# Packed softmax statistics, a spread over 128 rows and another order of the last tile in a three-mixer decoder trunk

## The chip, the cores and the metric

The kernel runs on one core of a Trainium2 chip. A core has five engines, each with a queue of its own: TensorE (PE; its weight loads are shown as PEld), VectorE (DVE), ScalarE (ACT), GpSimd (POOL) and SyncE (SP), which here issues the transfers. The metric is the device time in microseconds, median of three runs.

## The reference

A sequence of 512 rows of width 1024 goes through one layer: a root-mean-square norm, one wide projection, three mixers side by side, their gated sum and an output projection that is added to the input.

```
hn = rms_norm(x, ln_g[l])
proj = einsum('bsd,dc->bsc', hn, w_in[l])
qa, ka, va, ga, qb, kb, vb, gb, qc, kc, vc, gc, gate_logits = split(proj)
o_a = moba_attention(...)        # mixer A, 8 heads of 64
o_b = dilated_attention(...)     # mixer B, three groups of 8 heads
o_c = swa_sink_attention(...)    # mixer C, 8 heads, 2 for keys and values
branches = stack([o_a * silu(ga), o_b * silu(gb), o_c * silu(gc)])
br = einsum('bsiw,iwd->bsid', branches, w_branch[l])
x = x + einsum('bsd,de->bse', sum(sigmoid(gate_logits) * br), w_out[l])
```

Mixer B has three groups with (window, dilation) = (128, 1), (512, 4), (2048, 16). For each position and head the outputs of the groups are mixed by the softmax of their log-sum-exps, so the kernel needs from each group a maximum and a sum of exponentials for each position and head, and then one factor for each.

## The kernel before

All of the large products are made in three parts: a number is split into a high part and the rest (`whi`, `wlo` for a weight, `xhi`, `xlo` for the input), and high times high, low times high and high times low are added. So each column of a projection `pj` is made of triples of matmuls, lines 492, 493 and 494.

The input is normed in four token tiles of 128 rows. For each, ACT squares and sums (L208), DVE makes `rvx` (L141), POOL raises it to the power -0.5 (`rrx`, L143), DVE scales (`xn`, L213), PE transposes (L219, into `pt` and `xsc`), ACT and DVE split the result into `xhi` and `xlo` (L132, L137).

The mixers run in ten units, `A0 W0 R0 Z0 A1 W1 R1 Z1 C0 C1`: half the heads each, W, R and Z for the three groups of mixer B. The projection of the next unit is put between the steps of a unit. In what order the instructions stand on each engine is decided by a scheduler, which runs the kernel on its own estimates of durations; a changed instruction can move others that it has nothing to do with.

Softmax statistics lie in two tiles, `sl` (sums) and `sm` (minima of the negated maxima), of 128 rows by 4 token tiles by 96 columns: group W at columns 0 to 7, R at 32 to 39, Z at 64 to 71. R and Z compute their queries in a permuted order of tokens. After each third unit of mixer B comes a merge (L948 to L987): the statistics are transposed (`trs`, L953), copied back in the order of the tokens (`un`, L957), transposed again (`trb`, L960) and copied (L961); then come the factors. There are two merges, after Z0 and after Z1.

`spread` (L780 to L806) brings factors, one for each head and token, to the rows of the outputs: they are split into high and low parts in `ws`, transposed (L796), copied into a tile `wst`, and multiplied by a table of ones, `emat`, in a matmul `pb` (L805) with 64 rows of contraction. Groups 0 and 1 lie in the lower and upper 64 rows of one `wst`, group 2 in another. A and C call it with one value, the merge with three, so there are 20 matmuls `pb`.

The last projection keeps eight accumulators `acc`, one for each token tile and column half; it does the first six of eight slices of contraction for all of them, and then the last two, token tile by token tile (`out_mm`, L1084 to L1100). DVE adds the input to each half (`xr`, L1106) and SP stores it.

Of the kernel before, what the change touches and what calls it, by code (L numbers as in the profile page):

```python
# [9 lines left out]
F32 = mybir.dt.float32  # L10
F32R = mybir.dt.float32r
# [6 lines left out]
S = 512  # L18
D = 1024
NT = 4  # L20
KT = 8
# [4 lines left out]
ORAWS = 3  # L26
LAG = 2
KEEP = 0
UNITS = ("A0", "W0", "R0", "Z0", "A1", "W1", "R1", "Z1", "C0", "C1")
# [33 lines left out]
def shape_constants():  # L63
# [21 lines left out]
    ident[np.arange(128), 255 - np.arange(128)] = 1.0  # L85
    em = np.zeros((128, 512), np.float32)
    for g in range(4):
        for h in range(8):
            em[32 * g + h, h * 64 : (h + 1) * 64] = 1.0
    oh = np.concatenate([oh, oh])  # L90
# [10 lines left out]
def body(tc, x, ln_g, w_in, qk_g, sinks, w_branch, w_out, rel_bias, c_ident, c_onehot, c_mask, c_expand, out):  # L101
    nc = tc.nc
# [8 lines left out]
    with top:  # L111
# [7 lines left out]
        xlo = cp.tile([128, KT, S], F32R, name="xlo")  # L119
        emat = cp.tile([128, 512], F32R, name="emat")  # L120
        mhalf = cp.tile([128, 8], F32, name="mhalf")
# [104 lines left out]
        def start_bias():  # L226
# [9 lines left out]
            for kinds in (("A", "W"), ("C", "R", "Z")):  # L236
# [16 lines left out]
                nc.sync.dma_start(scr[:, c0 : c0 + n], fb[:, :n])  # L253
            e32 = qkv.tile([128, 512], F32, name="e32", tag="qn", bufs=3)
            nc.sync.dma_start(e32, c_expand)
            V.tensor_copy(emat, e32)

# [178 lines left out]
        with att:  # L436
# [7 lines left out]
            for c in range(0, 192, 32):  # L444
                G.tensor_copy(ws[:, :, c : c + 32], zer.rearrange("p (t c) -> p t c", t=NT))
            pthi = at.tile([128, 1664], F32R, name="pthi", bufs=1)
            ptlo = at.tile([128, 1664], F32R, name="ptlo", bufs=1)
# [333 lines left out]
            def spread(vals, hf, order, use):  # L781
# [9 lines left out]
                wst = []  # L791
                for g0 in range(0, ng, 2):
                    n = 64 * min(2, ng - g0)
                    tr = ps.tile([128, NT, 128], F32R, name="trs", tag="po")
                    for t in range(NT):
                        T.transpose(tr[:n, t], ws[:, t, 64 * g0 : 64 * g0 + n], order)  # L796
                    wt = at.tile([128, S], F32R, name="wst", tag="wst", bufs=2)
                    V.tensor_copy(wt[:n], tr[:n].bitcast(F32).rearrange("p a b -> p (a b)"))
                    wst.append(wt)
                for p in range(2):  # L800
                    for g in range(ng):
                        rows = slice(64 * (g % 2), 64 * (g % 2) + 64)
                        pb = ps.tile([128, 512], F32, name="pb", tag="po")
                        es = emat[rows, (hf * 2 + p) * 128 : (hf * 2 + p + 1) * 128]
                        T.matmul(pb, es, wst[g // 2][rows, :], start=True, stop=True)  # L805
                        use(p, g, pb)  # L806

            def stat_tile(tag, bufs):
                st = at.tile([128, NT, 96], F32, name=tag, tag=tag, bufs=bufs)
                G.memset(st, 0.0)  # L810
                return st

            def stat_fn(sl, sm, hf, g):
                def f(t, j):
                    c = 32 * g + hf * 4 + j
                    return sl[:, t, c : c + 1], sm[:, t, c : c + 1]

                return f
# [68 lines left out]
            for ui, (kind, hf, gi) in enumerate(units):  # L887
# [18 lines left out]
                else:  # L906
                    sl = stat_tile("sl", 2)
                    sm = sl[:, :, 32:]
                stat = stat_fn(sl, sm, hf, gi)
                steps = (residue_attention if kind in "RZ" else shared_attention if kind == "C" else pair_attention)(kind, hf, u, stat, oraw)  # L910
# [37 lines left out]
                elif len(bstate["o"]) == 3:  # L948

                    for s_ in (sl, sm):  # L950
                        tr = ps.tile([96, NT, 128], F32, name="trs", tag="po")
                        for t in range(NT):
                            T.transpose(tr[:, t], s_[:, t], rev)  # L953
                        un = at.tile([96, S], F32, name="un", tag="bt")
                        for g, pm in enumerate("NRR"):
                            rows = slice(32 * g, 32 * g + 32)
                            A.copy(perm_view(un[rows, :], pm), tr[rows])  # L957
                        tb = ps.tile([128, NT, 96], F32, name="trb", tag="po")
                        for t in range(NT):
                            T.transpose(tb[:, t], un[:, t * 128 : (t + 1) * 128], ident[:96, :96])  # L960
                        V.tensor_copy(s_, tb)  # L961
                    ln, mn = sl, sm
                    cs = [slice(32 * g + hf * 4, 32 * g + hf * 4 + 4) for g in range(3)]
                    mm = at.tile([128, NT, 4], F32, name="mm", tag="mm")
# [118 lines left out]
        wo = wnext  # L1083
        def out_mm(k, t):  # L1084
            tsl = slice(t * 128, (t + 1) * 128)
            for part, ws in ((mhi, (0, 1)), (mlo, (0,))):
                for e in range(2):
                    es = slice(e * 512, e * 512 + 512)
# [9 lines left out]
        for t in range(NT):  # L1098
            for k in range(KT - 2, KT):
                out_mm(k, t)  # L1100
        for t in range(NT):
# [29 lines left out]
```

## Time and profile before

| what | value |
|---|---|
| median of three runs | 805.29 us (805.21 to 806.34) |
| profiled execution | 808.76 us, its span 807.0 us |
| busy PE, DVE, ACT, POOL | 97%, 64%, 54%, 16% of the span |
| mean granted clock of TensorE | 0.987 |

The span reaches from the first to the last instruction of the profiled execution; 1.76 us of it lie outside. Busy shares are means over stages that differ, and PE is busy in nearly all of them.

### The profile page before, as it was taken

What the parts mean: (1) busy time and instruction counts of PE and PEld (TensorE: products, weight loads), DVE (VectorE), ACT (ScalarE), POOL (GpSimd) and SP (SyncE); (2) the same over time, 40 slices, a digit from 0 to 9 for tenths busy, and PEclk for the clock granted to TensorE, in tenths of its full rate; (3) what the DMA queues carried; (4) which work ended last, traced back from release to release, by engine and by line L of the source; (5) the groups of instructions that cost most, each with busy time, mean ns of one, the idle gap of its engine ahead of it and who ended that gap; (6) DMA issues with size and microseconds to landing.
All of it is one profiled execution on the core that took longest, in us unless ns stands there. A gap on an engine that the chain in (4) does not pass through costs nothing.

```text
span 807.0 us, 12636 instructions
## 1 busy us (share of the span) xinstructions
PE 783.0 (97%) x4727; PEld 663.4 (82%) x4727; DVE 515.6 (64%) x1088; ACT 432.4 (54%) x938; POOL 128.2 (16%) x90
## 2 busy tenths in 40 slices
PE   7999999999998999999999899999999999999997
PEld 4887887788878777878887787788899999999886
DVE  6765664564554667346554486848889887987512
ACT  5534564666577356447775865766355244445300
POOL 5422211112310340122032042100000000000000
PEclk9999999999998999999999699999999999999999
DMA  9443343351331153414431221414143334436302
GB/s 280 126 150 85 103 121 102 106 168 35 105 111 27 52 157 79 142 46 147 131 105 33 80 65 42 154 54 137 46 157 123 90 102 131 131 101 201 117 1 104
DMA packets 67328, 85.72 MB, mean 106 GB/s; under 512 B 4899, under 2 KB 53155, under 8 KB 67268
## 3 DMA queue, kind: packets, MB, share of 16 engines
q1 hardware_dynamic: 67268, 84.93, 34.2%
q8 instruction: 37, 0.61, 0.3%
q14 instruction: 23, 0.19, 0.1%
HBM read 75.41 MB, written 9.50 MB: 105 GB/s over the span
## 4 chain that ended last, share of the span: by engine, by line
PE 88%; DVE 4%; ACT 4%; issue 2%; DMA 1%; POOL 0%; SPq 0%; DVEq 0%; ACTq 0%; POOLq 0%
PE pj L492 13%; PE pj L493 12%; PE pj L494 12%; PE fc L352 10%; PE acc L1090 5%; PE fsc L352 4%; PE po L602 3%; PE sc L652 3%; PE pj L272 2%; PE pj L274 2%; PE pj L273 2%; PE po L1060 2%; PE po L1061 2%; PE po L1062 2%; PE tr L672 2%; PE tr L549 2%
## 5 line engine op out<-in xcount | busy, mean ns | idle before, releaser
L492 PE MATMUL pj<-whi,xhi 128*128 128x512 f32 (+1 forms) x576 | 203.9, 354 | 2.0 <-DVE whi L134 0.9
L493 PE MATMUL pj<-wlo,xhi 128*128 128x512 f32 (+1 forms) x576 | 199.2, 346 | 0.0
L494 PE MATMUL pj<-whi,xlo 128*128 128x512 f32 (+1 forms) x576 | 198.1, 345 | 0.0
L132 ACT CAST whi<-w 128x1024 fp32r<-128x1024 f32 x108 | 112.8, 1050 | 77.5 <-PE fsc L352 18.7
L137 DVE TENSOR_TENSOR wlo<-w,whi 128x1024 fp32r<-128x1024 f32 x93 | 117.6, 1273 | 39.1 <-ACT whi L132 38.4
L492 PEld LDWEIGHTS pj<-whi,xhi 128*128 128x128 f32 x576 | 111.0, 193 | 18.6 <-ACT xhi L132 1.7
L493 PEld LDWEIGHTS pj<-wlo,xhi 128*128 128x128 f32 x576 | 111.1, 193 | 12.4 <-issue 0.8
L494 PEld LDWEIGHTS pj<-whi,xlo 128*128 128x128 f32 x576 | 111.0, 193 | 12.4 <-issue 0.5
L143 POOL TENSOR_TENSOR rr<-rv,mhalf 128x8 f32<-128x8 f32 (+2 forms) x40 | 65.7, 1644 | 218.3 <-DVE rv L141 199.0
L137 DVE TENSOR_TENSOR ptlo<-tr,pthi 128x128 fp32r<-128x128 f32 (+3 forms) x112 | 50.9, 458 | 30.6 <-ACT pthi L132 22.4
L132 ACT CAST pthi<-tr 128x128 fp32r<-128x128 f32 (+3 forms) x112 | 44.4, 400 | 39.9 <-PE tr L672 19.5
L137 POOL TENSOR_TENSOR wlo<-w,whi 128x1024 fp32r<-128x1024 f32 x17 | 41.1, 2419 | 98.5 <-ACT whi L132 98.5
L519 DVE TENSOR_TENSOR qn<-qn,rr 128x512 f32<-128x512 f32 (+1 forms) x36 | 30.9, 858 | 32.9 <-POOL rr L143 32.8
L576 DVE CUSTOM_DVE_ANT_0 lg<-sc,bt 128x128 f32<-128x128 f32 (+2 forms) x96 | 28.5, 335 | 24.6 <-PE sc L652 12.2
L508 DVE TENSOR_REDUCE ss<-sq 128x8 f32<-128x512 f32 (+2 forms) x40 | 25.7, 642 | 28.8 <-ACT sq L506 28.4
L577 ACT ACTIVATE lg<-lg,sm 128x128 f32<-128x128 f32 (+1 forms) x80 | 32.8, 411 | 14.0 <-DVE sm L576 13.7
L352 PE MATMUL fc<-xlo,whi 128*128 128x256 f32 x144 | 40.2, 279 | 0.0
L352 PE MATMUL fc<-xhi,wlo 128*128 128x256 f32 x144 | 40.2, 279 | 0.0
L352 PE MATMUL fc<-xhi,whi 128*128 128x256 f32 x144 | 40.2, 279 | 0.0
L272 PE MATMUL pj<-xhi,whi 128*128 128x512 f32 x96 | 39.2, 408 | 0.0
L504 ACT COPY qn<-pj 128x512 f32<-128x512 f32 (+1 forms) x36 | 20.6, 571 | 33.3 <-PE pj L494 33.3
L273 PE MATMUL pj<-xlo,whi 128*128 128x512 f32 x96 | 37.9, 395 | 0.0
(259 smaller groups left out, 1752.7 us busy)
## 6 DMA issues: line engine op xcount, KB each, us to landing
w<-in_w_in SPq DMA_DIRECT2D x54, 512.0 KB, 4.2
w<-in_w_in SPq DMA_DIRECT2D x72, 256.0 KB, 3.8
w<-in_w_branch SPq DMA_DIRECT2D x12, 512.0 KB, 3.5
vscr<-vn SPq DMA_DIRECT2D x16, 256.0 KB, 2.8
w<-in_w_out SPq DMA_DIRECT2D x8, 512.0 KB, 4.6
osp<-oraw SPq DMA_DIRECT2D x6, 512.0 KB, 4.2
oback<-osp SPq DMA_DIRECT2D x6, 512.0 KB, 3.6
xt<-in_x SPq DMA_DIRECT2D x4, 512.0 KB, 6.6
```

Of the source, the lines that this page charges most:

```text
L132: A.copy(dst, src)
L137: eng.tensor_tensor(dst, src, hi.bitcast(F32), ALU.subtract)
L143: G.tensor_tensor(r, v, mhalf[:, :n], ALU.pow)
L272: T.matmul(psum, a, xhi[:, k, :], start=(k == 0), stop=False)
L273: T.matmul(psum, a, xlo[:, k, :], start=False, stop=False)
L352: T.matmul(psum[:, c], w[:, k, cs], x_[:, k, :], start=(first and c == 0 and k == 0 and q == 0), stop=(c == 1 and k == 3 and q == 2), skip ...
L492: T.matmul(pj[:, :ncol], xh, whi(k), start=(k == 0), stop=False)
L493: T.matmul(pj[:, :ncol], xh, wlo(k), start=False, stop=False)
L494: T.matmul(pj[:, :ncol], xl, whi(k), start=False, stop=(k == KT - 1))
L519: V.tensor_tensor(q3[:, :nq], q3[:, :nq], r[:, :nq].unsqueeze(2).broadcast_to([128, nq, 64]), ALU.mult)
L577: last_exp[0] = A.activation(lg, lg, AF.Exp, bias=mcol, scale=-1.0, accum_out=lcol)
L1090: T.matmul(acc[t * 2 + e], part[k // 2][:, k % 2, tsl], wo[q](k)[:, es], start=(k == 0 and q == 0 and part is mhi), stop=(k == KT - 1 and ...
```

## The change

There are three edits, and the order in which the scheduler then puts things.

First, `sl` and `sm` have 40 columns (`NST`) in place of 96: R at 0, Z at 8, W at 32 (`GCOL`). The two groups in permuted order are thus within the first 32 rows after the transpose, and one DVE copy with the permutation serves both; ACT copies 8 rows for W. The transposes `trb` have 40 rows of contraction and 40 columns in place of 96.

Second, `spread` contracts over all 128 rows. The table `emat` has two planes, one with ones in the lower and one with ones in the upper rows. `wst` is now two fixed tiles, whose upper 64 rows are cleared at the start by eight casts on POOL, because A and C fill the lower rows only. The table comes in two transfers with a DVE cast each.

Third, for the last token tile `out_mm` does the last two slices for one column half and then for the other.

```diff
+GCOL = (32, 0, 8)
+NST = 40
...
-    em = np.zeros((128, 512), np.float32)
+    em = np.zeros((128, 1024), np.float32)
     for g in range(4):
         for h in range(8):
-            em[32 * g + h, h * 64 : (h + 1) * 64] = 1.0
+            c = g // 2 * 512 + h * 64
+            em[32 * g + h, c : c + 64] = 1.0
...
-            e32 = qkv.tile([128, 512], F32, name="e32", tag="qn", bufs=3)
-            nc.sync.dma_start(e32, c_expand)
-            V.tensor_copy(emat, e32)
+            for g in range(2):
+                e32 = qkv.tile([128, 512], F32, name="e32", tag="qn", bufs=3)
+                nc.sync.dma_start(e32, c_expand[:, g * 512 : g * 512 + 512])
+                V.tensor_copy(emat[:, g], e32)
...
+            wsts = [at.tile([128, S], F32R, name=f"wst{i}", bufs=1) for i in range(2)]
+            for wt in wsts:
+                for c in range(0, S, 128):
+                    G.tensor_copy(wt[64:128, c : c + 128], zer[64:128, :])
...
-                    wt = at.tile([128, S], F32R, name="wst", tag="wst", bufs=2)
+                    wt = wsts[g0 // 2]
...
-                        rows = slice(64 * (g % 2), 64 * (g % 2) + 64)
                         pb = ps.tile([128, 512], F32, name="pb", tag="po")
-                        es = emat[rows, (hf * 2 + p) * 128 : (hf * 2 + p + 1) * 128]
-                        T.matmul(pb, es, wst[g // 2][rows, :], start=True, stop=True)
+                        es = emat[:, g % 2, (hf * 2 + p) * 128 : (hf * 2 + p + 1) * 128]
+                        T.matmul(pb, es, wst[g // 2], start=True, stop=True)
...
-                st = at.tile([128, NT, 96], F32, name=tag, tag=tag, bufs=bufs)
+                st = at.tile([128, NT, NST], F32, name=tag, tag=tag, bufs=bufs)
...
-                        tr = ps.tile([96, NT, 128], F32, name="trs", tag="po")
+                        tr = ps.tile([NST, NT, 128], F32, name="trs", tag="po")
                         for t in range(NT):
                             T.transpose(tr[:, t], s_[:, t], rev)
-                        un = at.tile([96, S], F32, name="un", tag="bt")
-                        for g, pm in enumerate("NRR"):
-                            rows = slice(32 * g, 32 * g + 32)
-                            A.copy(perm_view(un[rows, :], pm), tr[rows])
-                        tb = ps.tile([128, NT, 96], F32, name="trb", tag="po")
+                        un = at.tile([NST, S], F32, name="un", tag="bt")
+                        V.tensor_copy(perm_view(un[0:32, :], "R"), tr[0:32])
+                        A.copy(perm_view(un[32:NST, :], "N"), tr[32:NST])
+                        tb = ps.tile([128, NT, NST], F32, name="trb", tag="po")
                         for t in range(NT):
-                            T.transpose(tb[:, t], un[:, t * 128 : (t + 1) * 128], ident[:96, :96])
+                            T.transpose(tb[:, t], un[:, t * 128 : (t + 1) * 128], ident[:NST, :NST])
                         V.tensor_copy(s_, tb)
...
         for t in range(NT):
-            for k in range(KT - 2, KT):
-                out_mm(k, t)
+            if t < NT - 1:
+                for k in range(KT - 2, KT):
+                    out_mm(k, t)
+            else:
+                for e in range(2):
+                    for k in range(KT - 2, KT):
+                        out_mm(k, t, (e,))
```

In the order of the changed kernel, lines stand some 3 to 11 further down than before.

DVE at the start of the program, from its eighth instruction on, before (`w32_138` is the first weight tile; 110 and 136 are the first two token tiles):

```order
L141 TENSOR_SCALAR rvx_116<-xss_114 128x1
L213 SCALAR_TENSOR_TENSOR xn_120<-xt_110,rrx_118,lng_105 128x512
L213 SCALAR_TENSOR_TENSOR xn_120<-xt_110,rrx_118,lng_106 128x512
L141 TENSOR_SCALAR rvx_185<-xss_183 128x1
L134 CAST whi_141<-w32_138 128x1024
L213 SCALAR_TENSOR_TENSOR xn_189<-xt_136,rrx_187,lng_105 128x512
L137 TENSOR_TENSOR wlo_142<-w32_138,whi_141 128x1024
L213 SCALAR_TENSOR_TENSOR xn_189<-xt_136,rrx_187,lng_106 128x512
L137 TENSOR_TENSOR xlo_65<-pt_122,xhi_64 128x4x128
```

The same place of the changed kernel (`w32_148` is its first weight tile; 120 and 146 are the token tiles):

```order
L144 TENSOR_SCALAR rvx_126<-xss_124 128x1
L144 TENSOR_SCALAR rvx_195<-xss_193 128x1
L137 CAST whi_151<-w32_148 128x1024
L140 TENSOR_TENSOR wlo_152<-w32_148,whi_151 128x1024
L216 SCALAR_TENSOR_TENSOR xn_130<-xt_120,rrx_128,lng_115 128x512
L216 SCALAR_TENSOR_TENSOR xn_130<-xt_120,rrx_128,lng_116 128x512
L216 SCALAR_TENSOR_TENSOR xn_199<-xt_146,rrx_197,lng_115 128x512
L216 SCALAR_TENSOR_TENSOR xn_199<-xt_146,rrx_197,lng_116 128x512
L137 CAST whi_165<-w32_162 128x1024
L140 TENSOR_TENSOR xlo_65<-pt_132,xhi_64 128x4x128
L140 TENSOR_TENSOR wlo_166<-w32_162,whi_165 128x1024
```

The two `xn` of the first token tile have moved from the second place of this piece to behind `rvx` of the second tile and both halves of the first weight's split, and the cast of another weight stands ahead of `xlo`.

PE in the first merge, before (`po` is the last product of Z0, `pj_2714` and `pj_2743` are projections of the next units):

```order
L567 MATMUL po_2393<-pthi_97,vlo_1939 128x256
L953 MATMUL trs_2402<-idr_63,sl_1251 96x128 x4
L549 MATMUL tr_2542<-idr_63,qn_2526 128x128 x2
L494 MATMUL pj_2714<-whi_2271,xlo_65 128x256
L549 MATMUL tr_2583<-idr_63,qn_2572 128x128 x2
L492 MATMUL pj_2714<-whi_2271,xhi_64 128x256
L493 MATMUL pj_2714<-wlo_2272,xhi_64 128x256
L494 MATMUL pj_2714<-whi_2271,xlo_65 128x256
L960 MATMUL trb_2411<-idr_63,un_2407 128x96 x4
L953 MATMUL trs_2417<-idr_63,sm_1253 96x128 x4
L492 MATMUL pj_2743<-whi_2265,xhi_64 128x256
```

PE at the same place in the changed kernel (`pj_2722` and `pj_2751` are the same projections):

```order
L575 MATMUL po_2405<-pthi_107,vlo_1951 128x256
L960 MATMUL trs_2414<-idr_63,sl_1263 40x128 x4
L557 MATMUL tr_2550<-idr_63,qn_2534 128x128 x2
L502 MATMUL pj_2722<-whi_2283,xlo_65 128x256
L557 MATMUL tr_2591<-idr_63,qn_2580 128x128 x2
L500 MATMUL pj_2722<-whi_2283,xhi_64 128x256
L501 MATMUL pj_2722<-wlo_2284,xhi_64 128x256
L502 MATMUL pj_2722<-whi_2283,xlo_65 128x256
L500 MATMUL pj_2751<-whi_2277,xhi_64 128x256
L501 MATMUL pj_2751<-wlo_2278,xhi_64 128x256
...
L966 MATMUL trb_2422<-idr_63,un_2419 128x40 x4
L960 MATMUL trs_2428<-idr_63,sm_1265 40x128 x4
```

Where `trb` followed the projection's triple, the next projection now follows, and `trb` comes behind 23 of its matmuls and two more transposes.

ACT at that place, before (`qn_2664` is the copy that frees the buffer of an earlier projection):

```order
L778 COPY oraw_2275<-po_2393 64x2x128 x2
L957 COPY un_2407<-trs_2402 32x512
L957 COPY un_2407<-trs_2402 32x4x128 x2
L559 ACTIVATE khi_2497<-tr_2542,gn_71 128x2x128
L504 COPY qn_2664<-pj_2639 128x512
L559 ACTIVATE qhi_2495<-tr_2583,gq_72 128x2x128
```

ACT at the same place of the changed kernel, where that copy is `qn_2672`:

```order
L786 COPY oraw_2287<-po_2405 64x2x128 x2
L567 ACTIVATE khi_2505<-tr_2550,gn_71 128x2x128
L512 COPY qn_2672<-pj_2647 128x512
L567 ACTIVATE qhi_2503<-tr_2591,gq_72 128x2x128
L963 COPY un_2419<-trs_2414 8x512
```

The three copies `un` ahead of `khi` and `qn` are gone from there, and the one that is left stands behind them.

## Rows read from the trace of the kernel before

**Rows 1.** The page: span, and part 1, busy time by engine.

```profile
span 807.0 us, 12636 instructions
...
PE 783.0 (97%) x4727; PEld 663.4 (82%) x4727; DVE 515.6 (64%) x1088; ACT 432.4 (54%) x938; POOL 128.2 (16%) x90
```

**Rows 2.** PE's waits by releaser: total us, how many, longest us.

```profile
PE po L566 <- DVE ptlo L137: 3.3, 5, 2.1
PE trb L960 <- ACT un L957: 2.7, 1, 2.7
...
PE rp L232 <- DMA rb<-in_rel_bias: 0.4, 1, 0.4
```

**Rows 3.** Windows: length, busy by engine, then granted clock, DMA share, GB/s.

```profile
17.30:242.58 225.28, 220.47 (x1342) 182.64 (x1341) 132.65 (x328) 131.38 (x322) 53.52 (x32) 1.00 0.38 112
...
252.82:256.24 3.42, 3.42 (x19) 3.42 (x18) 1.39 (x5) 3.24 (x5) 1.64 (x1) 0.50 0.26 77
```

**Rows 4.** Timeline of the first merge: start, us, engine, instruction, idle before.

```profile
248.49 2.69 ACT L957 COPY un<-trs 32x512 f32<-32x512 f32 x3
251.21 0.47 ACT L559 ACTIVATE khi<-tr,gn 128x256 fp32r<-128x256 f32 x1
...
251.24 0.55 PE L960 MATMUL trb<-idr,un 96*128 96x96 f32 x4 [2.67 <-ACT un L957]
...
251.58 0.58 ACT L504 COPY qn<-pj 128x512 f32<-128x512 f32 x1
...
252.21 0.19 PEld L492 LDWEIGHTS pj<-whi,xhi 128*128 128x128 f32 x1 [0.23 <-ACT qn L504]
```

**Rows 5.** Timeline of PE around a single `pb`, in C1.

```profile
563.61 0.40 PE L1060 MATMUL po<-bp,whi 128*128 128x512 f32 x1
563.93 0.50 PE L805 MATMUL pb<-wst,emat 64*128 64x512 f32 x1
564.37 0.50 PE L1061 MATMUL fsc<-bp,whi 128*128 128x512 f32 x1
564.70 0.40 PE L1062 MATMUL fsc<-bp,wlo 128*128 128x512 f32 x1
564.94 0.40 PE L1060 MATMUL fsc<-bp,whi 128*128 128x512 f32 x1
```

**Rows 6.** Timeline of PE in the second merge: two neighbouring `pb`.

```profile
487.04 0.50 PE L805 MATMUL pb<-wst,emat 64*128 64x512 f32 x2
```

**Rows 7.** Instructions on tile `un`: ns least, median, most; first and last start.

```profile
L957 ACT COPY un<-trs x12: 557/1054/1083, 248.5 to 464.8; 32x512 f32<-32x512 f32 x12
```

**Rows 8.** Timeline of POOL at the start.

```profile
2.00 1.47 POOL L445 CAST ws<-zer 128x128 fp32r<-128x128 f32 x6
6.05 0.56 POOL L143 TENSOR_TENSOR rrx<-rvx,mhalf 128x1 f32<-128x1 f32 x1 [2.57 <-DVE rvx L141]
```

**Rows 9.** Timeline of PE and DVE at the start.

```profile
6.64 1.41 DVE L213 SCALAR_TENSOR_TENSOR xn<-xt,rrx,lng 128x512 f32<-128x512 f32 x2 [0.75 <-POOL rrx L143]
...
7.45 1.11 PE L219 MATMUL pt<-idr,xn 128*128 128x128 f32 x4 [1.39 <-DVE xn L213]
...
9.50 0.69 DVE L134 CAST whi<-w 128x1024 fp32r<-128x1024 f32 x1 [0.20 <-DMA w<-in_w_in]
...
10.34 0.77 PE L492 MATMUL pj<-whi,xhi 128*128 128x512 f32 x1 [0.92 <-DVE whi L134]
10.93 1.22 DVE L137 TENSOR_TENSOR wlo<-w,whi 128x1024 fp32r<-128x1024 f32 x1
...
13.45 0.63 PE L493 MATMUL pj<-wlo,xhi 128*128 128x512 f32 x1
...
13.87 0.63 PE L494 MATMUL pj<-whi,xlo 128*128 128x512 f32 x1
...
15.57 2.93 DVE L137 TENSOR_TENSOR wlo<-w,whi 128x1024 fp32r<-128x1024 f32 x1
```

**Rows 10.** Timeline of DVE at the end.

```profile
802.49 1.29 DVE L1106 TENSOR_TENSOR xr<-acc,xr 128x512 f32<-128x512 f32 x2 [1.28 <-PE acc L1090]
```

More of the change, by code (lines that the diff above doesn't have):

```diff
@@ L119, in body @@
         xlo = cp.tile([128, KT, S], F32R, name="xlo")
-        emat = cp.tile([128, 512], F32R, name="emat")
+        emat = cp.tile([128, 2, 512], F32R, name="emat")
         mhalf = cp.tile([128, 8], F32, name="mhalf")
@@ L814, in f @@
                 def f(t, j):
-                    c = 32 * g + hf * 4 + j
+                    c = g + hf * 4 + j
                     return sl[:, t, c : c + 1], sm[:, t, c : c + 1]
@@ L907, in body @@
                     sl = stat_tile("sl", 2)
-                    sm = sl[:, :, 32:]
-                stat = stat_fn(sl, sm, hf, gi)
+                    sm = sl[:, :, 16:]
+                stat = stat_fn(sl, sm, hf, GCOL[gi] if kind in "WRZ" else 0)
                 steps = (residue_attention if kind in "RZ" else shared_attention if kind == "C" else pair_attention)(kind, hf, u, stat, oraw)
@@ L950, in body @@
                     for s_ in (sl, sm):
-                        tr = ps.tile([96, NT, 128], F32, name="trs", tag="po")
+                        tr = ps.tile([NST, NT, 128], F32, name="trs", tag="po")
                         for t in range(NT):
                             T.transpose(tr[:, t], s_[:, t], rev)
-                        un = at.tile([96, S], F32, name="un", tag="bt")
-                        for g, pm in enumerate("NRR"):
-                            rows = slice(32 * g, 32 * g + 32)
-                            A.copy(perm_view(un[rows, :], pm), tr[rows])
-                        tb = ps.tile([128, NT, 96], F32, name="trb", tag="po")
+                        un = at.tile([NST, S], F32, name="un", tag="bt")
+                        V.tensor_copy(perm_view(un[0:32, :], "R"), tr[0:32])
+                        A.copy(perm_view(un[32:NST, :], "N"), tr[32:NST])
+                        tb = ps.tile([128, NT, NST], F32, name="trb", tag="po")
                         for t in range(NT):
-                            T.transpose(tb[:, t], un[:, t * 128 : (t + 1) * 128], ident[:96, :96])
+                            T.transpose(tb[:, t], un[:, t * 128 : (t + 1) * 128], ident[:NST, :NST])
                         V.tensor_copy(s_, tb)
                     ln, mn = sl, sm
-                    cs = [slice(32 * g + hf * 4, 32 * g + hf * 4 + 4) for g in range(3)]
+                    cs = [slice(g + hf * 4, g + hf * 4 + 4) for g in GCOL]
                     mm = at.tile([128, NT, 4], F32, name="mm", tag="mm")
@@ L1083, in body, with out_mm @@
         wo = wnext
-        def out_mm(k, t):
+        def out_mm(k, t, es_=(0, 1)):
             tsl = slice(t * 128, (t + 1) * 128)
             for part, ws in ((mhi, (0, 1)), (mlo, (0,))):
-                for e in range(2):
+                for e in es_:
                     es = slice(e * 512, e * 512 + 512)
```

## Prediction

> **What bounds the kernel now.** I read the page first: the matrix engine PE is busy for 783.0 of 807.0 us [rows 1], so time can leave only by making PE's instructions cheaper, by removing one of its waits, or by raising its clock. The list of what PE waited for comes next: it holds only a few waits near 2 us or more, and one of them, 2.7 us at the transposes `trb` behind ACT's copies `un`, stands in a place that the change rewrites [rows 2]. Then the windows by granted clock. PE ran at the full level of 2.4 GHz from 17.30 us on, but for a few stretches at 0.50 (1.2 GHz), of 3.42 us or a multiple of it; one of these, 252.82 to 256.24, begins 1.6 us after the long wait [rows 3, 4]. A stretch at 0.50 with PE always busy does half the work of one at 1.00, so it loses up to 1.7 us. Last I read the timeline around the `pb` matmuls, the first merge, the start and the tail.
>
> The profiled execution took 808.76 us for a span of 807.0 and the median is 805.29, so I take the sum against the span and put it on the median, as if both moved alike. A change under 0.2% (1.6 us) can't be told from none in this kernel.
>
> **The factors with all 128 rows.** A `pb` matmul uses 64 rows ("64*128"). Alone between two full matmuls, the steps from start to start are 0.32, 0.44 and 0.33 us (563.61, 563.93, 564.37, 564.70), where the next full step is 0.24 [rows 5]: the three take 1.09 instead of 0.72, so one trip into the half-row form and back costs 0.37, here called a trip. With 128 rows the `pb` should take the ordinary 0.24. Two neighbouring ones in different row halves lie side by side: such a pair is printed as one row of 0.50 us, as long as a single one [rows 6]. So a pair that stands together gains little from widening, and what is saved is the trips alone. The Trainium skill (TensorEngine Tiling (Array Packing), Key Properties) says that a change of tiling mode drains TensorE and that separate tiles run in parallel; the trace agrees with both, by 0.37 us and by the pair.
>
> I counted, in the order of PE, the unbroken stretches with fewer than 128 rows: 82 before, 73 after. Widening takes away one in A0, two in A1, four in the second merge and four in C0 and C1. In the first merge the wide `pb`s now cut a run of six score matmuls into five pieces where it was two, while three of the `pb`s' own stretches go, and the transposes `trb`, which have 40 rows in place of 96, open two new ones: two more there in all. In the second merge `trb` opens two, so two fewer remain. At the start two fewer, since score matmuls and the transposes `rp` now stand together. At 0.37 each: A0 -0.4, A1 -0.7, C0 and C1 -1.5, first merge +0.7, second merge -0.7, start -0.7. Bounds of one trip: 0.2 (a cut between neighbours that overlap anyway) to 0.5, so -1.8 to -4.5 for the nine, -3.3 taken.
>
> **The statistics moved together.** The transposes `trs` move the same 128 columns as before. `trb` moves 40 columns in place of 96: four took 0.55 us [rows 4], some 0.4 of it steps; at 40/96 I take off 0.2 a set, four sets, -0.7 in all (0 to -0.9). The copies are the larger part. Before, ACT made three for each set, 0.56 us in straight order and 1.05 to 1.08 in strided order [rows 7], in sum 2.69 from 248.49, and PE stood for 2.67 us, from 248.57 to 251.24 [rows 4]. After, ACT has one straight copy and DVE one strided one (0.7 to 1.4: my estimate from the straight and strided copies of ACT; DVE is idle for most of this stretch). More important is the order: the transposes that need `un` now come 25 instructions later, behind 23 matmuls of the next projection and two transposes. These need the buffer that ACT's copy `qn` frees, and ACT does `khi` (0.47) and `qn` (0.58) right after the `oraw` copies, so from 248.49 on, where `un` began before [rows 4]. PE should thus wait from 248.57 to some 249.54, 1.0 us, then run some 2.9 us of projection, by which time `un` (248.49 plus 1.05, a `qhi` as long as `khi`, and 0.56 on ACT, about 250.6) is long done. It waited 2.67 and then 0.23 for `qn`. Gain 2.90 - 1.0 = 1.9 us, bounds 0.9 (another wait near 1 us behind `qlo` or `qhi`) to 2.9.
>
> The fall of the clock at 252.82 followed the long wait. With a wait of 1.0 I take it as gone: -1.5 (0 to -1.7). A second merge without such a wait gains nothing by shorter copies: its `trb` shows none in the list of waits [rows 2].
>
> **The zero rows and the wider table.** The eight casts that clear rows 64 to 128 stand on POOL before its first square root `rrx`. Six casts of twice the rows took 1.47 us [rows 8], so the eight take at most 2.0, less what the smaller clearing of the statistics saves; POOL then stood idle for 2.57 us until DVE's `rvx` [rows 8]. Cost nothing; without that cover up to 2.0. The second piece of `emat` is one more load of 256 KB and one DVE cast off the critical path, with DVE at 64% [rows 1]: nothing, at most 0.4.
>
> **The order at the start.** The scheduler counts those casts as late, and so it has put DVE's `xn` of both first token tiles behind the split of the first weight. Before, `xn` ran at 6.64, at once after `rrx`, and PE transposed from 7.45 [rows 9]. The weight's cast `whi` ran 9.50 to 10.19. In the new order: `whi` to 10.2, `wlo` 1.22 more, to 11.4, then four `xn` of 0.71, to 14.2. PE transposes from 12.1; four took 1.11 us at this clock [rows 9], of which 0.85 is steps, so twelve bring it to about 14.8. The third matmul waits for `xlo`, which stands behind a second weight cast: about 16.0. By 17.30, from where the clock was up [rows 3], PE has done some 6 matmuls. Before it had done some 12: three from 10.34 on with waits between, then from 13.45 one per 0.42 us [rows 9]. Six times 0.24 is 1.4 us, and the next `wlo`, at 2.93 us [rows 9], ends about 0.2 after PE wants it: +1.6. Bounds +0.8 (the columns of transposes that were done later before) and +3.3 (the clock comes up 3.42 us later, half of it lost). `rp` moves ahead of some 24 matmuls of 0.12 us, while its load is issued only one weight earlier; it waited 0.4 [rows 2], and I take 0.5 more (0 to 2.5).
>
> **The last tile half by half.** DVE's two adds of the last token tile took 1.29 us from 802.49 [rows 10]. The second could start when the last matmul ends, one step of 0.24 after the first was released, about 802.73, but stood behind the first until about 803.1. With half 0 finished six matmuls ahead, the first is done early: -0.4 (0 to -0.6).
>
> **Sum.** Start +1.6 - 0.7 + 0.5 = +1.4; A0 -0.4; first merge -1.9 - 1.5 + 0.7 - 0.35 = -3.1; A1 -0.7; second merge -0.7 - 0.35 = -1.1; C0 and C1 -1.5; tail -0.4. Together -5.8 us: 799.5.
>
> **The rivals.**
> - *The clock falls again, or another wait takes the place of `un`'s.* PE still stands idle for 1.0 us in the first merge and waits on DVE close by are common (`ptlo`, 3.3 us in five [rows 2]). Then the 1.5 stay, and up to 0.9 of the wait: 801 to 802. For it: a stretch at half clock followed each of the long waits. Against: nothing else queues ahead of `qn` on ACT.
> - *The start takes more.* One mechanism, four `xn` behind the first weight split on DVE, with PE's first projection matmul moved from 10.34 to about 14.8 [rows 9]. If nothing of the old idle time is recovered, and the clock comes up one stretch later, 4.5 plus 1.7 stand for the 1.6 taken: 804.1, no change. It decides against the change from 7.4 us on, in place of the 1.6; with three late stretches it is 4.5 plus 5.1, 9.6: 807.5, slower. For it: all later work hangs on it and PE has no slack to catch up. Against: between 10.34 and 13.45 PE itself stood idle for much of the time, and that goes.
> - *Trips aren't what the half rows cost:* the 0.32 and 0.33 of the neighbours come from loading the next weights late, and stay with a wide `pb`. Then a trip is worth 0.2, and the nine give 1.8 in place of 3.3: 801.0. Against: the step before the `pb` is longer too, which loads nothing of it.
> - *The wide form gives up rows that ran side by side.* For the one pair that did [rows 6] that is 0.24. If all 20 had run so, ten times 0.24 would be lost and the trips would be no gain of the widening: -5.8 + 3.3 + 2.4, 805.2, no change. Against: 16 of the 20 stand alone in the order. The Trainium skill (TensorEngine Tiling (Array Packing), Theoretical Speedup) gives up to twice the speed for a contraction of 64 rows or fewer, which speaks against 128 rows; of the trace only that pair agrees.
> - *More goes with it*: short waits in A1 vanish with the new order, and `qn` is earlier: 797.5.
>
> **How the numbers follow.** Forecast 0.40; clock or a new wait 0.22; cheaper trips 0.12; more 0.10; start with no net change 0.08; slower by it 0.07; side-by-side rows 0.01. The range 797.0 to 803.5 leaves out most of the last two and the far end of "more". Faster by over 0.2% (under 803.7) takes the first four cases but for a few in 100, 0.80; within 0.2% 0.12; slower 0.08.
>
> **What would show it.** In the profile after: a `pb` form of 128*128 with steps of 0.24 around it; the wait of PE at `trb` gone and one near 1.0 at the projection behind `qn`; no stretch at 0.50 near 253 us; first projection matmul near 14.8 us and PE some seven matmuls late by 20 us; DVE's last add starting within 0.1 us of the last matmul's end. I am wrong if PE loses over 4 us before 50 us, if `trb` with 40 rows is dearer than with 96 by over 0.5 a set, or if new waits appear in A1, whose order changed too.

## The result and the profile after

The changed kernel takes 801.39 us (median of 4 runs, 799.48 to 801.84); the kernel before takes 805.82 in the same comparison. The ratio is 0.9947, 95% interval 0.9932 to 0.9961: 4.3 us less. Run again beside the experiments it came to 800.79 us and 0.9949 (0.9935 to 0.9964). The forecast was 799.5 in a range of 797.0 to 803.5.

The page of the changed kernel, its span and part 1 (the profiled execution took 801.84 us):

```profile
span 800.0 us, 12641 instructions
...
PE 772.4 (97%) x4727; PEld 658.0 (82%) x4727; DVE 518.0 (65%) x1093; ACT 425.5 (53%) x930; POOL 125.0 (16%) x98
```

Between the profiled executions [rows 1] the span is 7.0 us shorter and PE is busy for 10.6 us less, so the gain is in PE's busy time, and part of it is given back as idle time. Much of the 10.6 can be the clock: the execution of before spent 21.6 us at the lower level, that of the change 7.3, and at half the speed up to half of the difference, 7.2 us, is lost (my estimate). The medians differ by 4.4 us only; why is told below. Where PE waits, in the changed kernel (total us, how many, longest us):

```profile
PE pt L222 <- DVE xn L216: 5.7, 1, 5.7
PE po L574 <- DVE ptlo L140: 3.7, 6, 2.1
PE pj L500 <- ACT qn L512: 2.9, 4, 1.1
...
PE rp L235 <- DMA rb<-in_rel_bias: 0.6, 1, 0.6
```

The wait at `trb` [rows 2] is not in the list any more. In its place are a wait of 5.7 us at the start and two of about one us for `qn`. The timeline of the first merge, to be held against [rows 4]:

```profile
248.51 1.05 DVE L962 COPY un<-trs 32x512 f32<-32x512 f32 x1 [2.88 <-PE trs L960]
...
249.33 0.47 ACT L567 ACTIVATE khi<-tr,gn 128x256 fp32r<-128x256 f32 x1
249.71 0.58 ACT L512 COPY qn<-pj 128x512 f32<-128x512 f32 x1
...
250.34 0.39 PE L500 MATMUL pj<-whi,xhi 128*128 128x256 f32 x1 [0.95 <-ACT qn L512]
...
250.68 0.58 ACT L963 COPY un<-trs 8x512 f32<-8x512 f32 x1
...
253.20 0.28 PE L501 MATMUL pj<-wlo,xhi 128*128 128x256 f32 x1
```

PE waits 0.95 us for `qn`, then runs on; `un` is whole at 251.3, over 2 us before the transposes that read it, which follow the last row. A strided copy of 32 rows takes DVE 1.05 us, the same as ACT's.

The windows around that place in the changed kernel (length, busy by engine, then granted clock, DMA share, GB/s):

```profile
243.50:247.00 3.50, 3.50 (x20) 3.50 (x19) 1.18 (x2) 1.58 (x3) 0.00 (x0) 0.56 0.00 0
247.00:253.00 6.00, 5.05 (x44) 4.81 (x44) 3.20 (x7) 4.15 (x10) 0.00 (x0) 1.00 0.00 0
253.00:257.00 4.00, 4.00 (x37) 3.79 (x36) 3.04 (x7) 2.42 (x5) 1.64 (x1) 1.00 0.22 66
```

The first fall of the clock to the lower level (1.2 GHz) is still there; the second [rows 3] is gone. When the same kernel ran again (the fifth run), its trace had neither: the first fall comes and goes between executions of one kernel. A `pb` in C1, against [rows 5]:

```profile
557.97 0.39 PE L1066 MATMUL po<-bp,whi 128*128 128x512 f32 x1
558.20 0.39 PE L812 MATMUL pb<-wst,emat 128*128 128x512 f32 x1
558.43 0.40 PE L1067 MATMUL fsc<-bp,whi 128*128 128x512 f32 x1
558.66 0.40 PE L1068 MATMUL fsc<-bp,wlo 128*128 128x512 f32 x1
```

The form is 128*128 and every step is 0.23. But in the first merge the scheduler set wide `pb` between score matmuls of half rows:

```profile
284.33 0.38 PE L660 MATMUL sc<-khi,qhi 64*128 64x256 f32 x1
284.64 0.50 PE L812 MATMUL pb<-wst,emat 128*128 128x512 f32 x1
285.07 0.38 PE L660 MATMUL sc<-klo,qhi 64*128 64x256 f32 x1
285.38 0.50 PE L812 MATMUL pb<-wst,emat 128*128 128x512 f32 x1
285.82 0.38 PE L660 MATMUL sc<-klo,qhi 64*128 64x256 f32 x1
```

There the step of the wide matmul is 0.43 to 0.44, the same as that of a half-row `pb` between full matmuls before, and each score matmul takes a step of 0.31: the switch is paid either way.

The start of the changed kernel, against [rows 8] and [rows 9]:

```profile
6.08 0.56 POOL L146 TENSOR_TENSOR rrx<-rvx,mhalf 128x1 f32<-128x1 f32 x1 [1.19 <-DVE rvx L144]
...
8.78 0.15 DVE L144 TENSOR_SCALAR rvx<-xss 128x1 f32<-128x1 f32 x1 [2.85 <-ACT xsq L211]
...
9.88 1.23 DVE L140 TENSOR_TENSOR wlo<-w,whi 128x1024 fp32r<-128x1024 f32 x1
...
11.02 2.72 DVE L216 SCALAR_TENSOR_TENSOR xn<-xt,rrx,lng 128x512 f32<-128x512 f32 x4
...
11.82 1.12 PE L222 MATMUL pt<-idr,xn 128*128 128x128 f32 x4 [5.73 <-DVE xn L216]
...
14.29 0.78 PE L500 MATMUL pj<-whi,xhi 128*128 128x512 f32 x1
...
15.32 0.80 PE L502 MATMUL pj<-whi,xlo 128*128 128x512 f32 x1
...
18.00 0.39 PE L502 MATMUL pj<-whi,xlo 128*128 128x512 f32 x1
18.23 0.40 PE L500 MATMUL pj<-whi,xhi 128*128 128x512 f32 x1
```

POOL is not late: it stood idle for 1.19 us before its first `rrx`. DVE stood idle for 2.85 us, because the second tile's `rvx` is now next in its queue and ACT's squares for it were not there; with the old order it would have done the first tile's `xn` in that time. So PE's first transpose came 4.4 us later than before. From 18.00 us on PE's matmuls of 512 columns stand 0.23 us apart; up to 17.6 it was 0.42, the lower level of the clock.

The end of the changed kernel, against [rows 10]:

```profile
795.83 0.39 PE L1096 MATMUL acc<-whi,ml 128*128 128x512 f32 x1
...
796.26 0.69 DVE L1117 TENSOR_TENSOR xr<-acc,xr 128x512 f32<-128x512 f32 x1 [0.70 <-PE acc L1096]
```

The last add starts at 796.26, 0.04 us after the last matmul ends.

### The profile page after: what moved, and what is told of

Its sections match the earlier page's. It is cut to its first block, busy times and chain, and to the rows that moved or that the text cites. A ratio compares the mean times of both kernels' runs of the same rounds, so it can differ in the third digit from the quotient of the medians.

```text
span 800.0 us, 12641 instructions
## 1 busy us (share of the span) xinstructions
PE 772.4 (97%) x4727; PEld 658.0 (82%) x4727; DVE 518.0 (65%) x1093; ACT 425.5 (53%) x930; POOL 125.0 (16%) x98
## 4 chain that ended last, share of the span: by engine, by line
PE 87%; ACT 4%; DVE 4%; issue 2%; DMA 2%; SPq 1%; POOL 1%; DVEq 0%; POOLq 0%; ACTq 0%
PE pj L500 12%; PE pj L501 12%; PE pj L502 11%; PE fc L356 11%; PE acc L1096 6%; PE fsc L356 4%; PE po L610 3%; PE sc L660 3%; PE pj L278 2%; PE pj L276 2%; PE pj L277 2%; PE po L1066 2%; PE po L1067 2%; PE po L1068 2%; PE tr L680 2%
## 5 line engine op out<-in xcount | busy, mean ns | idle before, releaser
L146 POOL TENSOR_TENSOR rr<-rv,mhalf 128x8 f32<-128x8 f32 (+2 forms) x40 | 62.7, 1567 | 217.2 <-DVE rv L144 194.0
L278 PE MATMUL pj<-xhi,wlo 128*128 128x512 f32 x96 | 37.7, 393 | 0.0
```

The lines of the kernel that those rows point to most:

```text
L146: G.tensor_tensor(r, v, mhalf[:, :n], ALU.pow)
L278: T.matmul(psum, wlo(k)[:, c : c + 128], xhi[:, k, :], start=False, stop=(k == KT - 1))
```

## The experiments

Before all, which trace to compare with. The profiled execution of before was long for its kernel (808.76 us, the median is 805.3 to 805.8). The kernel of the fourth run differs from it only in the very last matmuls, and its trace passes the second merge 2.2 us sooner. So I compare with both, by the time at which PE starts the same instruction; the last column takes the changed kernel's other trace, that of the fifth run:

```
changed kernel minus    before    fourth run (tail only)    fifth run minus fourth
near 82 us              +1.25     +1.85                     +1.74
near 163 us (after A0)  +0.81     +1.47                     +1.44
near 341-363 (after A1) -2.48     -1.77                     -3.22
near 443                -2.48     -1.77                     -3.28
near 524 (after C0)     -5.64     -2.73                     -4.18
near 604 (after C1)     -6.45     -3.54                     -5.00
end of the span         -7.0      -3.6                      -5.0
```

With the tail's 0.4 the middle column comes to 4.0, near the measured 4.3. The 2.2 us by which the first two columns part between 443 and 524 lie where the execution of before ran at the lower clock for 13.7 us (447.38 to 461.04), the fourth run for 3.4. The fifth run gains what the change gains in every stretch but one: its 1.5 us more come at 243 us, where the first fall of the clock is missing.

The first four kernels are each compared with the kernel before.

**Wide factors alone** (`e1_spread`). Edit: the second part of the diff, on the statistics of before, whose tile is cut to 72 columns.

```diff
-                st = at.tile([128, NT, 96], F32, name=tag, tag=tag, bufs=bufs)
+                st = at.tile([128, NT, 72], F32, name=tag, tag=tag, bufs=bufs)
...
-                            rows = slice(32 * g, 32 * g + 32)
+                            rows = slice(32 * g, min(32 * g + 32, 72))
```

> Only the factors over 128 rows with their eight POOL casts, the statistics still in three places (their tile cut to the 72 columns in use, so that the larger table fits). Theory: the start loses 1.2 us as in the profile after, and twelve trips into the half-row form fewer outside the start, at 0.37 us, give 4.4: 3.2 us faster than before. Rival, that a trip is worth 0.2: 1.2 us faster. Rival, that the widening gives nothing and the packing all: 1.2 us slower.

Measured: 807.60 us, ratio 1.0029 (1.0014 to 1.0043), slower. The sign was missed. Against the fourth run's trace it is 4.6 us behind from 96 us on, and gains 3.3 us from there to the end, so the start took more than the factors gave. The start is not that of the change: here the scheduler put the cast of a second weight ahead of the second tile's `xn` as well, PE waited a further time, and its clock came up only at 23.4 us, as in the third run below.

**Packed statistics alone** (`e2_stats`). Edit: the first part of the diff and nothing else.

> Only the packed statistics; the start as before. Theory: PE's wait in the first merge falls from 2.9 to 1.0 us (-1.9), the stretch at half clock behind it goes (-1.5), the 40-column transposes give 0.7, and six more trips cost 2.2: 1.9 us faster. Rival, that the clock in that place has nothing to do with the wait: 0.4 us faster. Rival, that packing brings the whole gain: over 4 us faster.

Measured: 803.14 us, ratio 0.9971 (0.9960 to 0.9981), 2.3 us faster; the theory's sum of 1.9 holds and the two rivals fall. Its terms are not shown one by one by this. In its trace the wait at `trb` is gone and one of 0.95 for `qn` is there, as in the change.

**The casts alone** (`e3_casts`). Edit: fixed tiles with cleared upper rows, before's factors.

```diff
+            wsts = [at.tile([128, S], F32R, name=f"wst{i}", bufs=1) for i in range(2)]
+            for wt in wsts:
+                for c in range(0, S, 128):
+                    G.tensor_copy(wt[64:128, c : c + 128], zer[64:128, :])
...
-                    wt = at.tile([128, S], F32R, name="wst", tag="wst", bufs=2)
+                    wt = wsts[g0 // 2]
```

> Before, with only the two fixed tiles and the eight casts that clear their upper rows, which nothing reads as more than before; the scheduler's order at the start is nearly that of the change. Theory, that the order of DVE at the start costs: 1.2 to 1.6 us slower, PE's first transposes near 12 us. Rival, that the casts themselves are late on POOL: the power instruction after them starts later than 6.1 us. Rival, that the loss is made good later: no change.

Measured: 808.25 us, ratio 1.0044 (1.0029 to 1.0059), 2.9 to 3.5 us slower, twice what was expected. POOL at the start of this kernel, and then DVE:

```profile
3.54 1.98 POOL L449 CAST wst<-zer 64x128 fp32r<-64x128 f32 x8
6.79 0.56 POOL L143 TENSOR_TENSOR rrx<-rvx,mhalf 128x1 f32<-128x1 f32 x1 [1.27 <-DVE rvx L141]
```

```profile
10.32 1.40 DVE L213 SCALAR_TENSOR_TENSOR xn<-xt,rrx,lng 128x512 f32<-128x512 f32 x2
11.63 2.33 DVE L134 CAST whi<-w 128x1024 fp32r<-128x1024 f32 x1
13.88 1.39 DVE L213 SCALAR_TENSOR_TENSOR xn<-xt,rrx,lng 128x512 f32<-128x512 f32 x2
```

The casts are over at 5.52 and POOL waits 1.27 us for DVE after them, so the casts themselves cost nothing; `rrx` does start later than the rival's 6.1 us, at 6.79, but because `rvx` came late. The order they bring costs: as in the first run, and not as in the change, the second weight's cast stands between the two tiles' `xn`, and PE waited 6.5 us in two pieces (4.9 and 1.6). The clock is a second part of the loss. PE in this run:

```profile
22.58 0.63 PE L496 MATMUL pj<-whi,xhi 128*128 128x512 f32 x1
23.01 0.60 PE L497 MATMUL pj<-wlo,xhi 128*128 128x512 f32 x1
...
24.13 0.40 PE L496 MATMUL pj<-whi,xhi 128*128 128x512 f32 x1
24.36 0.39 PE L497 MATMUL pj<-wlo,xhi 128*128 128x512 f32 x1
```

The steps are 0.43 up to 23.4 us and 0.23 after it, where the change reached 0.23 at 18.0 and the fourth run at 15.8. In the first 90 us PE is idle for as long here as in the change (9.4 us each, summed from the traces), yet from 96 us on it is 1.3 us further behind the fourth run (3.05 us for 1.8). Of the twelve traces only those of this order, here and in the first run, have so late a clock; why it stays down is not shown. Eight instructions on an idle engine made the kernel some 3 us slower, through the order and what the order did to PE's waits and its clock. So this run does not price the start of the change, which has another order.

**The tail alone** (`e4_tail`). Edit: the third part of the diff.

> Only the last token tile half by half. Theory: DVE's last add starts at the end of the last matmul and the span is 0.4 us shorter, seen in the trace from the last matmul's start to the end of the span (4.76 us before). Rival, that the output transfer sets the end: the same 4.76 us.

Measured: 804.39 us, ratio 0.9992 (0.9976 to 1.0007), which can't be told from no change. The trace tells more than the time: from the start of the last matmul to the end of the span it takes 4.23 us (799.38 to 803.61; 4.21 in the change; 4.67 before, 802.29 to 806.95, and not the 4.76 of the expectation), so the tail is 0.43 us shorter, as expected. All seven traces with this edit have 4.21 to 4.23, all five without it 4.63 to 4.67.

The next four ran together.

**The change again** (`e5_after_again`), no edit.

> The changed kernel again, as the measure for the next three on the same chip: 4.4 us faster than before.

Measured: 800.79 us, ratio 0.9949 (0.9935 to 0.9964).

**The change without casts** (`e6_no_casts`). All 128 columns of the split factors are transposed each time, so nothing needs clearing.

```diff
-                    wt = wsts[g0 // 2]
-                    V.tensor_copy(wt[:n], tr[:n].bitcast(F32).rearrange("p a b -> p (a b)"))
+                    wt = at.tile([128, S], F32R, name="wst", tag="wst", bufs=2)
+                    V.tensor_copy(wt, tr.bitcast(F32).rearrange("p a b -> p (a b)"))
...
-                        T.transpose(tr[:n, t], ws[:, t, 64 * g0 : 64 * g0 + n], order)
+                        T.transpose(tr[:, t], ws[:, t, c0 : c0 + 128], order)
...
-                        es = emat[:, g % 2, (hf * 2 + p) * 128 : (hf * 2 + p + 1) * 128]
+                        es = emat[:, (g + 1) // 2, (hf * 2 + p) * 128 : (hf * 2 + p + 1) * 128]
```

> The change without the zero rows: the transposes bring 128 columns of the split factors each time (columns 0 to 127 for groups 0 and 1, 64 to 191 for group 2), so the upper rows hold finite numbers that meet zeros of the table, and no cast is needed. The scheduler then leaves the start as before. Theory, that the order at the start costs 1.2 us of the change: 1.2 us faster than the change, 5.6 us faster than before. Rival, that the start is made good by later waits: as the change.

Measured: 799.80 us, ratio 0.9939 (0.9923 to 0.9954). That is 1.0 us under the change, the size expected, but the intervals overlap. The traces at 82 us carry it: +0.6 us against the fourth run, where the change has +1.85. One execution parts from another by more than half of that: the seven traces with the start of before lie between -0.9 and +0.6 there (mean 0.0), the three with the change's start at +0.8, +1.7 and +1.85 (mean 1.5).

**Group W at column 64** (`e7_no_casts_w64`). The second transposes have 72 rows and thus the full form.

```diff
-GCOL = (32, 0, 8)
-NST = 40
+GCOL = (64, 0, 8)
+NST = 72
...
-                        V.tensor_copy(perm_view(un[0:32, :], "R"), tr[0:32])
-                        A.copy(perm_view(un[32:NST, :], "N"), tr[32:NST])
+                        V.tensor_copy(perm_view(un[0:64, :], "R"), tr[0:64])
+                        A.copy(perm_view(un[64:NST, :], "N"), tr[64:NST])
```

> The last one with group W at column 64 in place of 32, so that the second transposes of the statistics have 72 rows and take the full form (six trips fewer by the order). Theory, 0.37 us for a trip and 0.4 us more for the wider transposes: 1.8 us faster than without casts alone, 7.4 us faster than before. Rival, that half-row transposes cost no trip: 0.4 us slower than without casts alone.

Measured: 797.77 us, ratio 0.9906 (0.9891 to 0.9921): 7.6 us faster than before, 2.0 us faster than without casts alone (1.8 expected), and the best of all kernels here. The switch at the second transposes can be read off a set of four, here in the second merge, in the kernel before (96 rows), in the changed kernel (40) and in this one (72):

```profile
462.01 0.28 PE L494 MATMUL pj<-whi,xlo 128*128 128x256 f32 x1
462.13 0.50 PE L960 MATMUL trb<-idr,un 96*128 96x96 f32 x4
462.47 0.60 PE L953 MATMUL trs<-idr,sm 128*96 128x128 f32 x4
```

```profile
457.24 0.28 PE L501 MATMUL pj<-wlo,xhi 128*128 128x256 f32 x1
457.44 0.44 PE L966 MATMUL trb<-idr,un 40*128 40x40 f32 x4
457.81 0.61 PE L960 MATMUL trs<-idr,sm 128*40 128x128 f32 x4
```

```profile
452.82 0.28 PE L497 MATMUL pj<-wlo,xhi 128*128 128x256 f32 x1
452.94 0.42 PE L962 MATMUL trb<-idr,un 72*128 72x72 f32 x4
453.19 0.60 PE L956 MATMUL trs<-idr,sm 128*72 128x128 f32 x4
```

From the start of the matmul ahead to that of the next transpose it is 0.46, 0.57 and 0.37 us: 40 rows are dearer than 96, and 72 rows save 0.2 for a set, 0.8 at most for the four. Against the sixth run's trace this one gains 2.8 us between 243 and 363 us, the first merge and A1, and loses 1.0 again in the second merge. The order of other work moved there too: PE is idle for 1.4 us less. So the total is shown, and that it is the trips alone is not.

**Both copies on ACT** (`e8_copies_act`). The strided copy goes to ACT; all else as in the change.

```diff
-                        V.tensor_copy(perm_view(un[0:32, :], "R"), tr[0:32])
+                        A.copy(perm_view(un[0:32, :], "R"), tr[0:32])
```

> The change with the strided copy of the statistics on ACT in place of DVE; the scheduler then puts the second transposes where they were before. Theory, that the gain in the first merge is that ACT no longer stands between PE and its next projection: ACT has 1.05 plus 0.56 us of copies, PE waits about 1.6 us at these transposes and then 0.2 for the projection's buffer in place of 1.0 in all, so 0.8 us slower than the change, and up to 1.5 more if the clock falls. Rival, that the engine of the copies doesn't matter: as the change.

Measured: 801.16 us (798.11 to 802.92), ratio 0.9946 (0.9924 to 0.9967), as the change. The list of waits has the two waits at `trb`, 1.6 us in the first merge and 1.4 in the second:

```profile
PE trb L966 <- ACT un L963: 3.0, 2, 1.6
```

The time doesn't tell the two theories apart. The six runs are spread over 4.8 us, and in step with the mean granted clock: 798.11 and 798.33 us at 0.996, 802.92 at 0.989. The wait of 1.6 us was not followed by a fall in the profiled execution; in others the clock was lower. At a like clock the theory's 0.8 us is not seen: the two runs at 0.996 are shorter than all nine of the change (799.48 us at the least), and this trace, against the fifth run's, which has no fall in the first merge either, gains 1.6 us between 243 and 363 us.

**Wide factors without casts** (`e9_spread_no_casts`). Edit: the first run with the transposes of the sixth.

> The wide factors alone, as in the first run, but without the casts (128 columns transposed each time), so that the start stands as before. By the order there are 70 half-row stretches in place of 82, all twelve gone with the wide factor matmuls. Theory, 0.37 us for a trip: 4.4 us faster than before. Rival, 0.28, as the first run's trace gives outside its start: 3.3 us faster. Rival, that the loss of the first run is not the start but the wide matmuls: not faster.

Measured: 802.22 us, ratio 0.9966 (0.9951 to 0.9981), 2.7 us faster. Twelve trips at that are 0.23 us each (0.13 to 0.33 by the interval; the medians alone, 3.2 us apart, would give 0.26). The theory's 4.4 and its 0.37 fall, the rival's 3.3 stays possible, and the last rival falls: the loss of the first run was its start. Against the fourth run's trace next to nothing is gained up to 443 us, where four of the twelve stretches went, then 1.4 us in the second merge and C0 for six, and 0.6 in C1 for two.

The parts, each taken alone, add up to the change: statistics -2.3, wide factors -2.7, the casts' order +1.0 (the fifth run less the sixth), the tail -0.4, together -4.4 for the -4.3 measured; each of the first three is known to about 1 us.

**Group W at 64, both copies on ACT** (`e10_w64_act`). The edits of the seventh and of the eighth run together.

> The change without casts and with group W at column 64, and both statistics copies on ACT. The scheduler puts the second transposes early, as before. Theory from the eighth run's trace: PE waits 1.6 us there in place of 1.0 a little later, no fall of the clock, and the work behind is earlier: within 1 us of the same kernel with the strided copy on DVE, either way. Rival, that ACT's queue is what costs: 1 to 2.5 us slower than that one.

Measured: 801.60 us, ratio 0.9957 (0.9940 to 0.9975), 3.8 us slower than the seventh, whose interval lies apart. Here the rival had the sign, and the loss is more than it said: with the copies on ACT the second transposes stand early and PE waits for them in both merges (3.0 us in all, as in the eighth run), and its runs spread again, from 798.95 us at 0.995 to 803.75 at 0.987, though two at 0.995 and 0.996 took 801.70 and 800.83. That the waits are the cause is not shown, since the same waits cost the eighth run nothing against the change. The traces of this run and the seventh put 0.9 us of the difference at the start, where both kernels have one order, and 2.6 in the first merge and A1, where the order of other work differs. What ACT's queue costs stays open.

## Why the prediction was right, and where it was off

The direction, the range and most of the mechanisms held; the sum of -5.8 us was larger than the 4.3 measured. Of the 1.9 us between 799.5 and 801.39 another 0.5 is the kernel before itself, 805.82 in this comparison for 805.29.

**The start**: +1.4 forecast, +1.25 against before's trace, +1.85 against the fourth run's. `xn` ended at 13.7 for 14.2 forecast, PE's first projection matmul started at 14.29 for 14.8, the third waited for `xlo` to 15.32 for 16.0; `rp` waited 0.2 us more for 0.5. The sixth run, without the casts, shows that this is the casts' doing through the order, and the rows of the third run that POOL is not late by them. The rival in which the clock comes up later did not come about here (17.9 us for 17.3 before); it did in the first and third runs.

**The first merge and A1**: -3.8 forecast (-3.1 and -0.7), -3.3 against before and -3.2 against the fourth run. The wait went from 2.67 and 0.23 us to 0.95, as worked out (1.0). The stretch at the lower clock went with it: it follows the 2.7 us wait in the traces of before and of the first, third, fourth and ninth runs, and is missing after the 0.95 us wait in the change, both times, and in the second, sixth and seventh runs, and after the 1.6 us wait of the eighth and tenth. That the wait brings the fall is consistent with all twelve and was not tried by a wait alone. New waits took back part of A1, which the prediction had named as a sign of being wrong; the longest:

```profile
315.13 0.50 PE L812 MATMUL pb<-wst,emat 128*128 128x512 f32 x1
316.71 0.38 PE L500 MATMUL pj<-whi,xhi 128*128 128x256 f32 x1 [1.08 <-ACT qn L512]
```

This is the changed kernel: its next projection stands right behind the `pb` and waits for `qn`, which is behind other work on ACT. Over the first merge and A1 together, summed from the traces, PE is idle for 5.3 us where the fourth run has 6.1. So of the -3.2 only 0.8 is waiting, for the 1.9 that the wait alone was to give; up to 1.7 is the clock (3.4 us fewer at the lower level), and about 0.7 the rest. That the stretch came out near the forecast is in part luck.

**The second merge and C0**: -1.85 forecast (-1.1 and half of the -1.5), about -1.0 against the fourth run (from -1.77 to -2.73). **C1**: -0.75 forecast, -0.8 measured. **The tail**: -0.4 forecast, -0.43 measured.

**The term that was mis-sized** is the trip at 0.37 us, nine of which were to give 3.3. The price was read where a `pb` stands alone between full matmuls, and it holds there: the two in C1 gave 0.8 (0.6 in the ninth run). But stretches of half rows were counted as if all cost the same. In the ninth run twelve of them were worth 2.7 us, 0.23 each on average and less than that before the second merge; in the change wide `pb`s between score matmuls pay the switch still (rows of 284 us above), and a set of `trb` pays 0.2 for its own. Nine at 0.23 are 2.1, which makes the sum -4.6. That is near the size measured; it is an average and not the price of each place. A second term went with it: 40 columns in place of 96 were to save 0.2 us a set, but the steps within a set fell only from 0.08 to 0.06 us, which is 0.08 a set, and 72 columns have the same 0.06. The two errors partly cancelled: a set was to cost 0.2 us more, narrower transposes and switch together, and costs 0.1. The rival with 0.2 for a trip, given 12 in 100, was nearer in its size; its reason, late weight loads next to a wide matmul, was not what the rows show, since the steps beside a wide `pb` in C1 are 0.23.

**The step from span to median** failed too, without harm to the number: the text put the sum against the profiled span "as if both moved alike". They moved by 7.0 and 4.4, because the profiled execution of before had the lower clock for longer than most of its other runs (mean 0.987; of the 32 run beside the first experiments three are as low).

## What to carry to other kernels

Price a switch of TensorE's row form where the changed instruction will stand, not where it stood: beside full-form matmuls it was worth 0.3 to 0.4 us here, at a set of small transposes 0.2, and a wide matmul set between half-row ones still paid it. A wait that PE meets behind a busy engine can be shortened by letting independent matmuls stand ahead of what waits; count then what PE waits for next, since here over half of the 1.9 us won at one place was lost again at others. Where a scheduler orders by its own estimates, look at the order of the first microseconds after any edit, and at when the clock comes up: eight casts on an idle engine cost about 1 us in one order and some 3 in another.

## What the runs showed of the hardware

The granted clock varies from run to run of one kernel, and its time goes with it: the eighth kernel took 798.1 to 802.9 us with a mean clock of 0.996 to 0.989. The two traces of the changed kernel differ by one fall of 3.4 us in the first merge, and by 1.4 us in their spans. A profiled execution can be one of the longer ones, by 3 us here. The figure alone is not enough: the ninth run's trace is printed at 0.95 where the others have 1.00, and its matmuls in C1 still stand 0.23 us apart.

The strided copy of 32 rows by 512 took 1.05 us on DVE and 1.05 on ACT, so nothing is won by the engine itself. Transposes `trb` of 40 rows take little less than those of 96, which have 246 ns each at the median before:

```profile
L966 PE MATMUL trb<-idr,un x16: 198/230/252, 253.4 to 462.2; 40*128 40x40 f32 x16
```

That is 230 ns each at the median in the changed kernel, where the kernel of the seventh run has 226 with 72 rows. With the steps around it, a set of four is cheapest at 72 rows (0.37 us for 0.46 and 0.57, rows at the seventh run).
